# A hand-written TensorE order for the first column tiles of a four-sublayer diffusion backbone, with squares and modulated inputs shared differently between VectorE and ScalarE

## The chip, the cores and the metric

The kernel runs on one core of a Trainium2 chip. The metric is the device time of one execution in microseconds. TensorE (PE) does the matmuls, PEld is its weight load, VectorE is DVE, ScalarE is ACT, and SyncE (SP) issues the transfers. Times inside an execution are counted from the first instruction of its profile.

## The reference

Two layers work on 256 latent tokens and 256 context tokens of width 1024. What matters here is the very beginning of layer 0:

```python
mod_l = [m[..., None, :] for m in jnp.split(sc @ w_ada[l] + b_ada[l], 6, axis=-1)]   # sc = silu(c)
mod_c = [m[..., None, :] for m in jnp.split(scc @ w_ada[l] + b_ada[l], 6, axis=-1)]  # scc = silu(c_ctx)
hl = rms_norm(x, norm1_gain[l]) * (1.0 + mod_l[1]) + mod_l[0]
hc = rms_norm(z, norm1_gain[l]) * (1.0 + mod_c[1]) + mod_c[0]
... even_mixer(hc @ w_in_even[j], hl @ w_in_even[j], ...)
```

So each token is divided by its root mean square over the 1024 features, each feature is scaled and shifted by numbers that come from a product with `w_ada`, and the result `h` is multiplied by the wide input weight. Attention, two gated scans and two SwiGLU blocks follow; the change leaves their code alone.

## The kernel before, in words

Features lie on the partitions. The 1024 features make eight tiles `x[0]` to `x[7]` of 128 partitions by 512 tokens (256 context, 256 latent). In the instruction lists `x_86` or `x0_86` is `x[0]`, `x_88` is `x[1]`, and so on to `x_100`, which is `x[7]`.

**Precision.** Every dense product is made of three matmuls (`mm3`, L275): a float32 operand is split into a rounded high part and the low rest, and high times high, high times low and low times high are added. For weights, `wpiece` (L263) loads a 0.5 MB piece of eight 128x128 blocks into `w`, ScalarE rounds it to `wH` (L269) and VectorE subtracts to get `wL` (L270). There are four buffers of each. `Flat` (L280) hands the blocks out in order.

**The first stage** (L400 to L434) does this, for all eight feature tiles:

- 30 idle matmuls on `ones` (`keep_warm`, L397; a second call runs 6 on `rsd` later).
- Squares of the eight `x` tiles on ScalarE, four buffers; VectorE adds them in pairs; four matmuls with `ones` sum over the partitions into `nms`. `rstd_from_ms` (L254) takes Ln and then Exp on ScalarE; the result `rsd` is named `nrs` in the trace.
- The modulation of feature tile `dt` (`ada_first`, L182, through `ada_two`, L151): 16 small matmuls of `sc` with a 1 MB piece of `w_ada` (called the sums below; the trace counts 32 instructions), a copy `ada_ev` on ScalarE (L159), two transposes on TensorE (L161), and three small operations on VectorE that leave shift and scale in `modt` (L162, L165, L168).
- For each feature tile `k`: `x[k]` times `rsd` on VectorE (L424), scale and shift by halves on ScalarE (L427), rounding to `hH` on ScalarE (L429), subtraction to `hL` on VectorE (L430), then 18 matmuls of 512 columns: three for each of six output column tiles `pss[0]` to `pss[5]`, all accumulated over `k`. These six are the first column tiles.

Six weight pieces `w_even_a` serve this stage: piece 0 holds the blocks for `k` = 0 and the first two of `k` = 1, piece 1 goes on from there, and so on.

**The order.** Within an engine, instructions run in the order of the program. That order is made at build time by a scheduler that works with its own estimate of durations; `after` (L55) and `high_priority` only bend it. All transfers are issued from SP's queue, in an order that the scheduler also sets. Eight semaphores are handed to the transfers in turn, and a transfer is issued only once the one that had its semaphore before has landed.

Of the kernel before, what the change touches and what calls it, by code (L numbers as in the profile page):

```python
# [10 lines left out]
F32 = mybir.dt.float32  # L11
F32R = mybir.dt.float32r
U32 = mybir.dt.uint32
AF = mybir.ActivationFunctionType
ALU = mybir.AluOpType
# [3 lines left out]
P = 128  # L19
D = 1024  # L20
KT = D // P
NC_ = 256
T = 512
# [9 lines left out]
HOLD0 = (-1, -1, 1, 3)  # L33
HOLD1 = (-1, 1, 2, 4)
WARM1 = 30
WARM2 = 6
OUT = (KT, P, 256)
JOINT = "natural_log_exp_and_others"

# [11 lines left out]
def hybrid_kernel(ctx: ExitStack, tc: tile.TileContext, A, out, dbg=None):  # L51
    nc = tc.nc
    PE, V = nc.tensor, nc.vector

    def after(ins, deps):  # L55
        for d in deps:
            tc.add_manual_dep(
                ins.ins, d.ins.name, mybir.DependencyInfo(mybir.DependencyClass.NoSync, mybir.DependencyReason.DATA),
                reason="table order",
            )  # L60
# [27 lines left out]
    S = Act()  # L88

    def pool(es, name, bufs, **kw):  # L90
        kw.setdefault("reuse_waits", "tile")
        return es.enter_context(tc.tile_pool(name=name, bufs=bufs, **kw))

    cst = pool(ctx, "cst", 1)
# [9 lines left out]
    def dma(o, i):  # L104
        nc.sync.dma_start(out=o, in_=i)

    def load(name, shape, dt=F32, p=None):
        t = (p or cst).tile(list(shape), dt, name="c_" + name)
        dma(t, A[name])
        return t  # L110
# [5 lines left out]
    def mm(o, l, r, start, stop):  # L116
        return PE.matmul(out=o, lhsT=l, rhs=r, start=start, stop=stop)  # L117

    def mtile(name, tag):
        return pm.tile([P, 512], F32, name=name, tag=tag, bufs=1 if tag == "t" else 2)  # L120


    cc = load("cc", (P, KT, 2))
    ones = cst.tile([P, P], F32, name="ones")
    V.memset(ones, 1.0)
    x = {}
# [7 lines left out]
    ident = cst.tile([P, P], F32, name="ident")  # L134
    bada = cst.tile([P, 2, 6, KT], F32, name="bada")
    ngain = cst.tile([P, 2, 2, KT], F32, name="ngain")
    eps_t = cst.tile([P, 1], F32, name="eps_t")
    V.memset(eps_t, EPS)
    one_t = cst.tile([P, 1], F32, name="one_t")
# [7 lines left out]
    acoef = {}  # L147

    modt = mp.tile([P, 2, 6, KT, 2], F32, name="modt")

    def ada_two(ws, md, bias, gain, tag):  # L151

        ps = dtile() if tag == "d" else mtile("ada_ps", tag)
        for i, w in enumerate(ws):
            for j in range(2):
                for g in range(4):
                    mm(ps[32 * g:32 * g + 32, i * P:(i + 1) * P], sc[:, 2 * g + j, :], w[:, 2 * g + j, :], j == 0, j == 1)
        ev = mp.tile([P, 2 * P], F32, name="ada_ev", tag="ada_ev", bufs=2)
        S.copy(out=ev, in_=ps[:, 0:2 * P])  # L159
        for i in range(2):  # L160
            PE.transpose(ps[:, (2 + i) * P:(3 + i) * P], ev[:, i * P:(i + 1) * P], ident)  # L161
        V.tensor_reduce(  # L162
            out=md, in_=ps[:, 2 * P:4 * P].rearrange("p (i g r) -> p i r g", i=2, g=4)[:, :, 0:2, :], axis=AX.X, op=ALU.add
        )
        V.tensor_tensor(out=md, in0=md, in1=bias.unsqueeze(2).to_broadcast([P, 2, 2]), op=ALU.add)  # L165
        if gain is not None:
            md, gain = gain
            V.scalar_tensor_tensor(out=md, in0=md, scalar=1.0, in1=gain, op0=ALU.add, op1=ALU.mult)  # L168
# [7 lines left out]

    def ada_load(dt):
        w = nps.tile([P, 2, KT, P], F32, name="ada_w0", tag="ada_w0", bufs=4)
        dma(w, A["w_ada"][0, 0:2, dt].rearrange("m p k c -> p m k c"))
        return w  # L180

    def ada_first(dt, w):  # L182

        ada_two([w[:, 0], w[:, 1]], modt[:, 0, 0:2, dt, :], bada[:, 0, 0:2, dt],
                (modt[:, 0, 1, dt, :], ngain[:, 0, 0, dt:dt + 1].to_broadcast([P, 2])), "at"[dt % 2])

    pending = [(m, dt) for m in (2, 4, 3) for dt in range(0, KT, 2)]

# [55 lines left out]
    def halves(n):  # L244
        return ((0, 0, 256), (1, 256, 512)) if n == 512 else ((1, 0, 256),)

    def h_tiles(k, n, name, hpool):
        return (hpool.tile([P, n], F32R, name=f"{name}H{k}", tag=f"hH{k}"),
                hpool.tile([P, n], F32R, name=f"{name}L{k}", tag=f"hL{k}"))

    def shift(l, which, k, v):
        return mods[l, 3 * which, k][:, v:v + 1]

    def rstd_from_ms(o, ps, n):  # L254

        S.activation(out=o, in_=ps, func=AF.Ln, scale=1.0 / n, bias=eps_t)
        S.activation(out=o, in_=o, func=AF.Exp, scale=-0.5)
# [17 lines left out]
    def mm3(o, aH, aL, bH, bL, first, last):  # L275
        mm(o, aH, bH, first, False)
        mm(o, aH, bL, False, False)
        mm(o, aL, bH, False, last)
# [75 lines left out]
    def dtile():  # L354
        return pd.tile([P, 512], F32, name="d", tag="d")
# [3 lines left out]
    nps = pool(nes, "nps0", 2)  # L359
# [35 lines left out]
    def keep_warm(n, rhs):  # L395
        for _ in range(n):
            mm(idle[:, 0:rhs.shape[1]], ones, rhs, True, True)  # L397

    keep_warm(WARM1, ones)
    ms = mtile("nms", "s")  # L400
    for k in range(0, KT, 2):
        sq = [nps.tile([P, T], F32, name="nsq", tag="nsq", bufs=4) for _ in range(2)]
        for i in range(2):
            S.activation(out=sq[i], in_=x[k + i], func=AF.Square)
        V.tensor_tensor(out=sq[0], in0=sq[0], in1=sq[1], op=ALU.add)
        mm(ms, ones, sq[0], k == 0, k == KT - 2)
    rsd = nps.tile([P, T], F32, name="nrs0", tag="nrs0", bufs=1)
    rstd_from_ms(rsd, ms, D)
    keep_warm(WARM2, rsd[:, 0:256])
    aw = ada_load(0)  # L410
    dma(ident, A["ident"])
    dma(bada, A["b_ada"])
    dma(ngain, A["ngain"])
    fl = Flat(A["w_even_a"])
    fl.fetch()
    ada_first(0, aw)
    ada_first(1, ada_load(1))
    pss = [dtile(), dtile(), dtile(), mtile("d3", "s"), mtile("d4", "s"), mtile("d5", "a")]
    h = {}
    prev = []  # L420
    for k in range(KT):
        if 1 <= k < KT - 1:
            ada_first(k + 1, ada_load(k + 1))
        after(V.tensor_tensor(out=x[k], in0=x[k], in1=rsd, op=ALU.mult), prev)  # L424
        h[k] = h_tiles(k, T, "h", hp)
        for v, lo, hi in halves(T):
            xs = x[k][:, lo:hi]  # L427
            S.activation(out=xs, in_=xs, func=AF.Identity, scale=acoef[0, 0, k][:, v:v + 1], bias=shift(0, 0, k, v))
            S.copy(out=h[k][0][:, lo:hi], in_=xs)  # L429
            prev = [V.tensor_tensor(out=h[k][1][:, lo:hi], in0=xs, in1=h[k][0][:, lo:hi], op=ALU.subtract)]  # L430
        for ps in pss:
            wH, wL = fl.nxt()
            mm3(ps, wH, wL, h[k][0], h[k][1], k == 0, k == KT - 1)
    nes.close()  # L434
    hf = dict(x)

    mk32 = load("mk32", (P, 64), U32)
    mks = load("mks", (P, 5, 32), U32)
    gains = load("gains", (P, 3))
    onesw = one_t.to_broadcast([P, 256])  # L440
# [358 lines left out]
    for j in range(4):  # L799
        gs[j] = bigp.tile([P, T], F32, name=f"gs{j}", tag=f"vB{j}")  # L800
        ps = dtile()
# [17 lines left out]
    nps = pool(nes, "nps", 2)  # L819
# [12 lines left out]
    def close_norm(fl, rhs, ks, l, m, xs, ssq, nl, which):  # L832


        hs = {k: h_tiles(k, T, "h", hp2) for k in range(KT)}

        def part(v, ps):
            lo, hi = halves(T)[v][1:]
            for i, j in enumerate((KT - 2, KT - 1)):
                V.scalar_tensor_tensor(  # L840
                    out=xs[j][:, lo:hi], in0=ps[:, i * 256:(i + 1) * 256], scalar=mods[l, m, j][:, v:v + 1],
                    in1=xs[j][:, lo:hi], op0=ALU.mult, op1=ALU.add,
                )
# [16 lines left out]
    pss = [dtile(), dtile(), dtile(), mtile("d3", "t")]  # L860
# [64 lines left out]
    h = ffn(0, T, h, x, gpool, ssq, A["w_ffn_in0"], A["w_ffn_out0"])  # L925
# [213 lines left out]
    h = {k: h_tiles(k, 256, "h", hp2) for k in range(KT)}  # L1139
# [161 lines left out]
```

## Time and profile before

| what | value |
|---|---|
| three timed runs | 1173.56, 1174.69, 1174.72 us; median 1174.69 |
| the profiled execution | 1171.33 us, its span 1169.6 us |
| TensorE busy | 1146.2 us, 98% of the span |
| VectorE, ScalarE busy | 794.5 us (68%), 546.6 us (47%) |
| mean granted TensorE clock | 0.991 |
| end of the first column tiles on TensorE | 66.7 us from the start |

The profiled execution is 3.36 us shorter than the median of the timed runs. A timeline row reads: start, length, engine, line, operation, result and operands, and in brackets how long the engine sat idle before it and what ended that. Neighbouring instructions overlap a little, so the pitch of a series is shorter than the length of one.

### The profile page before, as it was taken

The page shows a single profiled execution, that of the slowest core. Times are in us where ns is not written, and L with a number is a line of the kernel's source. Part 1 is how long each engine was busy: PE and PEld are TensorE (multiplying, and loading weights), DVE is VectorE, ACT ScalarE, POOL GpSimd, SP SyncE. Part 2 cuts the span into 40 slices and gives each one's busy share as a digit, 9 for nine tenths or more (in the row PEclk, how much of TensorE's full clock was granted, in tenths as well). Part 3 has the DMA queues.
Part 4 walks back from the last instruction along what each step waited for, and adds up shares of the span by engine and source line. Part 5 has one row for each costly group of instructions (what it writes and reads, how often), then busy time and mean ns, then how long its engine had stood idle before and what let it go on. Part 6 is the DMA issues. An engine that isn't in the chain of part 4 may idle for free. (4 is left out here: it accounts for less than half of the span.)

```text
span 1169.6 us, 21851 instructions
## 1 busy us (share of the span) xinstructions
PE 1146.2 (98%) x8954; PEld 982.8 (84%) x8954; DVE 794.5 (68%) x1671; ACT 546.6 (47%) x952; POOL 0.2 (0%) x4
## 2 busy tenths in 40 slices
PE   8999999999999999999999999999999998999998
PEld 6777665666889888888888889999898988999998
DVE  3537856985767767666677637869899976655663
ACT  5436546754435222212222325958778865433432
POOL 0000000000000000000000000000000000000000
PEclk9999989999999999999999999999999999999999
DMA  9531432234423555555776422342221234555552
GB/s 356 211 116 36 146 127 82 100 127 146 178 74 105 167 178 171 159 174 179 252 238 232 161 90 70 129 145 92 73 91 61 87 127 129 183 191 178 185 181 91
DMA packets 50021, 170.19 MB, mean 146 GB/s; under 512 B 6528, under 2 KB 8064, under 8 KB 49792
## 3 DMA queue, kind: packets, MB, share of 16 engines
q1 hardware_dynamic: 49920, 168.79, 43.2%
q8 instruction: 70, 1.15, 0.4%
q14 instruction: 31, 0.25, 0.1%
HBM read 167.72 MB, written 1.05 MB: 144 GB/s over the span
## 5 line engine op out<-in xcount | busy, mean ns | idle before, releaser
L269 ACT CAST wH<-w 128x1024 fp32r<-128x1024 f32 x212 | 222.2, 1049 | 410.2 <-PE d L117 314.0
L117 PE MATMUL d<-hL,wH 128*128 128x256 f32 (+1 forms) x1152 | 386.7, 336 | 2.5 <-DVE hL L387 2.5
L117 PE MATMUL d<-hH,wH 128*128 128x256 f32 (+1 forms) x1152 | 382.4, 339 | 5.6 <-ACT hH L71 4.1
L117 PE MATMUL d<-hH,wL 128*128 128x256 f32 (+1 forms) x1152 | 385.3, 335 | 0.0
L270 DVE TENSOR_TENSOR wL<-w,wH 128x1024 fp32r<-128x1024 f32 x212 | 258.6, 1221 | 124.7 <-ACT wH L269 122.0
L117 PEld LDWEIGHTS d<-hH,wH 128*128 128x128 f32 x1152 | 218.3, 191 | 32.0 <-ACT hH L71 4.9
L117 PEld LDWEIGHTS d<-hL,wH 128*128 128x128 f32 x1152 | 220.6, 191 | 25.0 <-DVE hL L387 3.3
L117 PEld LDWEIGHTS d<-hH,wL 128*128 128x128 f32 x1152 | 220.1, 191 | 21.5
L117 PE MATMUL d<-gL,wH 128*128 128x256 f32 (+1 forms) x374 | 121.8, 327 | 0.0
L117 PE MATMUL d<-gH,wL 128*128 128x256 f32 (+1 forms) x374 | 121.7, 327 | 0.0
L117 PE MATMUL d<-gH,wH 128*128 128x256 f32 (+1 forms) x374 | 121.7, 327 | 0.0
L227 DVE SCALAR_TENSOR_TENSOR jk<-ada_w,scb 128x1024 bf16<-128x1024 f32 x80 | 97.7, 1222 | 2.2 <-DMA ada_w<-in_w_ada 0.8
L882 DVE TENSOR_TENSOR fs<-fs,d 128x256 f32<-128x256 f32 (+1 forms) x46 | 24.6, 536 | 77.4 <-PE d L117 75.8
L117 PEld LDWEIGHTS d<-gL,wH 128*128 128x128 f32 x374 | 71.1, 190 | 6.1
L117 PEld LDWEIGHTS d<-gH,wL 128*128 128x128 f32 x374 | 71.1, 190 | 6.0
L117 PEld LDWEIGHTS d<-gH,wH 128*128 128x128 f32 x374 | 71.0, 190 | 6.0
L117 PE MATMUL d<-wH,hH 128*128 128x256 f32 (+1 forms) x192 | 61.9, 323 | 0.0
L117 PE MATMUL d<-wL,hH 128*128 128x256 f32 (+1 forms) x192 | 61.6, 322 | 0.0
L117 PE MATMUL d<-wH,hL 128*128 128x256 f32 (+1 forms) x192 | 61.5, 321 | 0.0
L825 DVE SCALAR_TENSOR_TENSOR x<-d,modt,x 128x256 f32<-128x256 f32 x64 | 28.5, 480 | 42.4 <-PE d L117 42.4
L71 ACT ACTIVATE QK<-QK 128x512 f32<-128x512 f32 x72 | 42.6, 628 | 2.4 <-DVE QK L493 2.1
L117 PEld LDWEIGHTS a<-QK 128*32 128x32 f32 (+5 forms) x1408 | 33.8, 118 | 10.1 <-issue 6.3
(216 smaller groups left out, 1461.1 us busy)
## 6 DMA issues: line engine op xcount, KB each, us to landing
w<-in_w_ffn_in SPq DMA_DIRECT2D x88, 512.0 KB, 3.4
ada_w<-in_w_ada SPq DMA_DIRECT2D x80, 512.0 KB, 4.2
w<-in_w_ffn_out SPq DMA_DIRECT2D x44, 512.0 KB, 3.4
ada_w<-in_w_ada SPq DMA_DIRECT2D x8, 1024.0 KB, 9.4
w<-in_w_even_a SPq DMA_DIRECT2D x16, 512.0 KB, 4.8
w<-in_w_odd_f SPq DMA_DIRECT2D x16, 512.0 KB, 3.3
x<-in_xT SPq DMA_DIRECT2D x16, 256.0 KB, 3.7
w<-in_w_out_even SPq DMA_DIRECT2D x8, 512.0 KB, 3.5
```

The source lines that it names most:

```text
L71: ins = nc.scalar.activation(**kw)
L117: return PE.matmul(out=o, lhsT=l, rhs=r, start=start, stop=stop)
L227: ins = V.scalar_tensor_tensor(out=jk, in0=w1[0], scalar=1.0, in1=scb[:, v, :], op0=ALU.mult, op1=ALU.mult, accum_out=modt[:, l, m, dt, v: ...
L269: S.copy(out=wH, in_=w)
L270: ins = V.tensor_tensor(out=wL, in0=w, in1=wH, op=ALU.subtract)
L825: tail[0] = V.scalar_tensor_tensor(out=xt[:, lo:hi], in0=ps[:, lo:hi], scalar=mods[l, m, k][:, v:v + 1], in1=xt[:, lo:hi], op0=ALU.mult, o ...
L882: V.tensor_tensor(out=s[:, lo:hi], in0=s[:, lo:hi], in1=pu, op=ALU.mult)
```

## The change

- TensorE's order is taken out of the scheduler's hands from the first idle matmul to the last matmul of the first column tiles (`manual_schedule`): it is the order of the code. The other engines' orders still come from the scheduler.
- `ada_two` is cut in `ada_sums` and `ada_turn`. The sums of tile `k + 2` stand in the middle of the matmuls of tile `k`, as do the turn (transposes and VectorE's three operations) and `h` of tile `k + 1`.
- Squares 1, 4 and 6 are made by VectorE, the other five by ScalarE; every square has a buffer of its own, and five instead of four matmuls sum them.
- Scale and shift of `h` move from ScalarE to VectorE; `hL` is one operation of 512 columns instead of two of 256.
- `cc`, `ident`, `b_ada` and `ngain` are issued from ScalarE's queue; each 1 MB piece of `w_ada` is loaded in two transfers.
- Six idle matmuls on `rsd` become two on the last square and three on `rsd`.

```diff
+    def dma_act(o, i):
+        nc.scalar.dma_start(out=o, in_=i)
...
-    cc = load("cc", (P, KT, 2))
+    cc = cst.tile([P, KT, 2], F32, name="c_cc")
+    dma_act(cc, A["cc"])
...
+    dma_act(ident, A["ident"])
+    dma_act(bada, A["b_ada"])
+    dma_act(ngain, A["ngain"])
...
     def ada_load(dt):
         w = nps.tile([P, 2, KT, P], F32, name="ada_w0", tag="ada_w0", bufs=4)
-        dma(w, A["w_ada"][0, 0:2, dt].rearrange("m p k c -> p m k c"))
+        for m in range(2):
+            dma(w[:, m], A["w_ada"][0, m, dt])
         return w
...
+    ordered = ExitStack()
+    ordered.enter_context(tc.manual_schedule(engines={PE.engine}))
     keep_warm(WARM1, ones)
     ms = mtile("nms", "s")
-    for k in range(0, KT, 2):
-        sq = [nps.tile([P, T], F32, name="nsq", tag="nsq", bufs=4) for _ in range(2)]
-        for i in range(2):
-            S.activation(out=sq[i], in_=x[k + i], func=AF.Square)
-        V.tensor_tensor(out=sq[0], in0=sq[0], in1=sq[1], op=ALU.add)
-        mm(ms, ones, sq[0], k == 0, k == KT - 2)
+    sq = [nps.tile([P, T], F32, name=f"nsq{k}", tag=f"nsq{k}", bufs=1) for k in range(KT)]
+    for k in range(KT):
+        if k in (1, 4, 6):
+            V.tensor_tensor(out=sq[k], in0=x[k], in1=x[k], op=ALU.mult)
+        else:
+            S.activation(out=sq[k], in_=x[k], func=AF.Square)
+    for k in (0, 2, 4):
+        V.tensor_tensor(out=sq[k], in0=sq[k], in1=sq[k + 1], op=ALU.add)
+    for k in (0, 2, 4, 6, 7):
+        mm(ms, ones, sq[k], k == 0, k == KT - 1)
     rsd = nps.tile([P, T], F32, name="nrs0", tag="nrs0", bufs=1)
     rstd_from_ms(rsd, ms, D)
-    keep_warm(WARM2, rsd[:, 0:256])
...
+    first_sums(0)
+    keep_warm(2, sq[KT - 1][:, 0:256])
+    first_turn(0)
+    keep_warm(3, rsd[:, 0:256])
...
+    def first_h(k):
+        V.tensor_tensor(out=x[k], in0=x[k], in1=rsd, op=ALU.mult)
+        h[k] = h_tiles(k, T, "h", hp)
         for v, lo, hi in halves(T):
             xs = x[k][:, lo:hi]
-            S.activation(out=xs, in_=xs, func=AF.Identity, scale=acoef[0, 0, k][:, v:v + 1], bias=shift(0, 0, k, v))
+            V.tensor_scalar(out=xs, in0=xs, scalar1=acoef[0, 0, k][:, v:v + 1], scalar2=shift(0, 0, k, v),
+                            op0=ALU.mult, op1=ALU.add)
             S.copy(out=h[k][0][:, lo:hi], in_=xs)
-            prev = [V.tensor_tensor(out=h[k][1][:, lo:hi], in0=xs, in1=h[k][0][:, lo:hi], op=ALU.subtract)]
-        for ps in pss:
+        V.tensor_tensor(out=h[k][1], in0=x[k], in1=h[k][0], op=ALU.subtract)
+
+    first_h(0)
+    for k in range(KT):
+        if k + 2 < KT:
+            aws[k + 2] = ada_load(k + 2)
+        for j, ps in enumerate(pss):
+            if k == 0 and j == 2:
+                first_sums(1)
+            if j == (4 if k == 0 else 2):
+                if k + 1 < KT:
+                    first_turn(k + 1)
+                    first_h(k + 1)
+                if k + 2 < KT:
+                    first_sums(k + 2)
             wH, wL = fl.nxt()
             mm3(ps, wH, wL, h[k][0], h[k][1], k == 0, k == KT - 1)
+    ordered.close()
```

The names below carry buffer numbers; `x0` to `x7` are the feature tiles, `hH0` and `hL0` the two parts of `h[0]`, `nrs0` is `rsd`.

VectorE, from the first weight subtraction on, before:

```order
L270 TENSOR_TENSOR wL_190<-w_187,wH_189 128x1024
L162 TENSOR_REDUCE modt_112<-ada_ps_193 128x2x2
L424 TENSOR_TENSOR x0_86<-x0_86,nrs0_172 128x512
L165 TENSOR_TENSOR modt_112<-modt_112,bada_103 128x2x2
L168 SCALAR_TENSOR_TENSOR modt_112<-modt_112,ngain_104 128x2
L430 TENSOR_TENSOR hL0_251<-x0_86,hH0_250 128x256 x2
L424 TENSOR_TENSOR x1_88<-x1_88,nrs0_172 128x512
```

and in the changed kernel:

```order
L287 TENSOR_TENSOR wL_187<-w_184,wH_186 128x1024
L445 TENSOR_TENSOR x0_86<-x0_86,nrs0_177 128x512
L445 TENSOR_TENSOR x1_88<-x1_88,nrs0_177 128x512
L445 TENSOR_TENSOR x2_90<-x2_90,nrs0_177 128x512
L445 TENSOR_TENSOR x3_92<-x3_92,nrs0_177 128x512
L445 TENSOR_TENSOR x4_94<-x4_94,nrs0_177 128x512
L445 TENSOR_TENSOR x5_96<-x5_96,nrs0_177 128x512
L445 TENSOR_TENSOR x6_98<-x6_98,nrs0_177 128x512
L445 TENSOR_TENSOR x7_100<-x7_100,nrs0_177 128x512
L174 TENSOR_REDUCE modt_115<-ada_ps_193 128x2x2
L177 TENSOR_TENSOR modt_115<-modt_115,bada_103 128x2x2
L180 SCALAR_TENSOR_TENSOR modt_115<-modt_115,ngain_104 128x2
```

All eight products with `rsd` now stand ahead of the first tile's scale and shift; before, only that of `x[0]` did.

ScalarE, from the last square to the rounding of `h[1]`, before:

```order
L71 ACTIVATE nsq_167<-x7_100 128x512
L269 CAST wH_189<-w_187 128x1024
L71 ACTIVATE nrs0_172<-nms_147,eps_t_105 128x512
L159 COPY ada_ev_210<-ada_ps_193 128x256
L71 ACTIVATE nrs0_172<-nrs0_172 128x512
L71 ACTIVATE x0_86<-x0_86,modt_112 128x256 x2
L429 CAST hH0_250<-x0_86 128x256 x2
L269 CAST wH_319<-w_317 128x1024
L159 COPY ada_ev_236<-ada_ps_219 128x256
L269 CAST wH_384<-w_382 128x1024
L159 COPY ada_ev_295<-ada_ps_278 128x256
```

and in the changed kernel:

```order
L70 ACTIVATE nsq7_160<-x7_100 128x512
L286 CAST wH_186<-w_184 128x1024
L70 ACTIVATE nrs0_177<-nms_152,eps_t_108 128x512
L70 ACTIVATE nrs0_177<-nrs0_177 128x512
L168 COPY ada_ev_210<-ada_ps_193 128x256
L451 CAST hH0_229<-x0_86 128x256 x2
L286 CAST wH_351<-w_349 128x1024
L286 CAST wH_416<-w_414 128x1024
L286 CAST wH_484<-w_482 128x1024
L168 COPY ada_ev_262<-ada_ps_245 128x256
L168 COPY ada_ev_300<-ada_ps_283 128x256
L451 CAST hH1_276<-x1_88 128x256 x2
```

The rounding of weight piece 0 stays ahead of Ln (the first `nrs0` row); the roundings of pieces 1, 2 and 3 now all stand ahead of `ada_ev_262`, the copy that the second tile's transposes need.

TensorE, in the middle of tile 0, before:

```order
L117 MATMUL d5_248<-hH0_250,wL_190 128x512
L117 MATMUL ada_ps_278<-ada_w0_276,sc_109 32x128 x8
L161 MATMUL ada_ps_219<-ident_102,ada_ev_236 128x128 x2
L117 MATMUL ada_ps_278<-ada_w0_276,sc_109 32x128 x8
L117 MATMUL ada_ps_337<-ada_w0_335,sc_109 32x128 x16
L161 MATMUL ada_ps_278<-ident_102,ada_ev_295 128x128 x2
L161 MATMUL ada_ps_337<-ident_102,ada_ev_354 128x128 x2
L117 MATMUL d_243<-hH1_303,wH_189 128x512
```

and in the changed kernel:

```order
L119 MATMUL d3_225<-hH0_229,wL_187 128x512
L173 MATMUL ada_ps_245<-ident_102,ada_ev_262 128x128 x2
L119 MATMUL ada_ps_283<-ada_w0_236,sc_112 32x128 x16
L119 MATMUL d4_226<-hH0_229,wH_186 128x512
L119 MATMUL d4_226<-hL0_230,wH_186 128x512
L119 MATMUL d4_226<-hH0_229,wL_187 128x512
L119 MATMUL d5_227<-hH0_229,wH_186 128x512
```

Before, the sums and transposes for the next tiles came in one block after tile 0's matmuls; now the transposes of tile 1 and the sums of tile 2 stand ahead of tile 0's last six matmuls.

## Rows read from the trace of the kernel before

**Rows 1.** The page's first part: busy time, share and instructions of each engine.

```profile
PE 1146.2 (98%) x8954; PEld 982.8 (84%) x8954; DVE 794.5 (68%) x1671; ACT 546.6 (47%) x952; POOL 0.2 (0%) x4
```

**Rows 2.** Busy time of engines by stretch; last three columns: clock, DMA share, GB/s.

```profile
5.00:10.00 5.00, 5.00 (x45) 4.89 (x44) 2.08 (x3) 4.08 (x8) 0.00 (x0) 1.00 1.00 358
...
20.00:25.00 5.00, 5.00 (x53) 3.59 (x54) 1.68 (x2) 1.32 (x2) 0.00 (x0) 1.00 1.05 401
...
45.00:50.00 5.00, 5.00 (x43) 3.79 (x42) 1.22 (x1) 1.41 (x2) 0.00 (x0) 1.00 0.29 93
```

**Rows 3.** Timeline of TensorE, first 73 us: start, length, line, operation, idle before.

```profile
13.46 1.12 PE L117 MATMUL nms<-nsq,ones 128*128 128x512 f32 x2
...
16.03 0.44 PE L161 MATMUL ada_ps<-ident,ada_ev 128*128 128x128 f32 x2 [1.10 <-ACT ada_ev L159]
16.56 2.86 PE L117 MATMUL idle<-nrs,ones 128*128 128x256 f32 x12
19.42 1.65 PE L117 MATMUL d<-hH,wH 128*128 128x512 f32 x6
21.00 1.08 PE L117 MATMUL ada_ps<-ada_w,sc 128*32 128x128 f32 x32
...
29.45 0.44 PE L161 MATMUL ada_ps<-ident,ada_ev 128*128 128x128 f32 x2 [1.67 <-ACT ada_ev L159]
...
58.45 1.52 PE L117 MATMUL d<-hH,wH 128*128 128x512 f32 x6
...
62.53 1.52 PE L117 MATMUL d<-hH,wH 128*128 128x512 f32 x6
...
66.71 0.38 PE L117 MATMUL lps<-lpr,ones 64*128 64x2 f32 x2
...
72.91 1.92 PE L117 MATMUL lr_ps<-x,c_w_lr 128*32 128x512 f32 x16
```

**Rows 4.** Timeline of ScalarE, first 30 us.

```profile
14.08 1.04 ACT L269 CAST wH<-w 128x1024 fp32r<-128x1024 f32 x1 [2.70 <-DMA w<-in_w_even_a]
15.03 0.68 ACT L71 ACTIVATE nrs<-nms,eps_t 128x512 f32<-128x512 f32 x1
15.61 0.36 ACT L159 COPY ada_ev<-ada_ps 128x256 f32<-128x256 f32 x1
15.86 0.64 ACT L71 ACTIVATE nrs<-nrs 128x512 f32<-128x512 f32 x1
...
18.67 0.69 ACT L429 CAST hH<-x 128x256 fp32r<-128x256 f32 x2
...
25.89 1.05 ACT L269 CAST wH<-w 128x1024 fp32r<-128x1024 f32 x1 [2.56 <-DMA w<-in_w_even_a]
```

**Rows 5.** Timeline of SP's queue, first 14 us: issues of transfers.

```profile
0.73 0.39 SPq L105 DMA_DIRECT2D c_cc<-in_cc  x1
1.18 3.74 SPq L105 DMA_DIRECT2D x<-in_xT  x8
```

**Rows 6.** Timeline of VectorE, first 54 us.

```profile
15.16 1.23 DVE L270 TENSOR_TENSOR wL<-w,wH 128x1024 fp32r<-128x1024 f32 x1 [3.05 <-ACT wH L269]
...
16.68 0.69 DVE L424 TENSOR_TENSOR x<-x,nrs 128x512 f32<-128x512 f32 x1
...
19.09 0.76 DVE L430 TENSOR_TENSOR hL<-x,hH 128x256 fp32r<-128x256 f32 x2 [1.45 <-ACT hH L429]
...
51.35 0.17 DVE L162 TENSOR_REDUCE modt<-ada_ps 128x4 f32<-128x16 f32 x1 [3.83 <-PE ada_ps L161]
51.55 0.17 DVE L165 TENSOR_TENSOR modt<-modt,bada 128x4 f32<-128x4 f32 x1
51.75 0.16 DVE L168 SCALAR_TENSOR_TENSOR modt<-modt,ngain 128x2 f32<-128x2 f32 x1
```

**Rows 7.** Groups of VectorE's instructions by line and shape: busy us, mean ns.

```profile
L765 DVE TENSOR_SCALAR p<-p,st 128x256 f32<-128x256 f32 x8 | 2.7, 343 | 0.0
```

**Rows 8.** Stretches with a lower granted clock; columns as in rows 2.

```profile
162.00:163.00 1.00, 0.26 (x2) 0.12 (x1) 0.90 (x6) 1.00 (x5) 0.00 (x0) 0.50 0.74 299
163.00:164.00 1.00, 0.76 (x2) 0.67 (x3) 0.90 (x5) 0.62 (x1) 0.00 (x0) 0.50 0.97 389
...
171.00:172.00 1.00, 1.00 (x4) 0.75 (x3) 0.73 (x4) 0.23 (x1) 0.00 (x0) 0.50 0.45 61
172.00:173.00 1.00, 1.00 (x6) 0.82 (x5) 0.17 (x1) 0.79 (x4) 0.00 (x0) 0.90 0.87 311
```

More of the change, by code (lines that the diff above doesn't have):

```diff
@@ L35 @@
 WARM1 = 30
-WARM2 = 6
 OUT = (KT, P, 256)
@@ L151, in ada_two, with ada_sums @@
     def ada_two(ws, md, bias, gain, tag):
+        ada_turn(*ada_sums(ws, tag), md, bias, gain)
+    def ada_sums(ws, tag):
         ps = dtile() if tag == "d" else mtile("ada_ps", tag)
@@ L159, in ada_two, with ada_turn @@
         S.copy(out=ev, in_=ps[:, 0:2 * P])
+        return ps, ev
+    def ada_turn(ps, ev, md, bias, gain):
         for i in range(2):
@@ L178, in ada_load, with first_sums, first_turn @@
         w = nps.tile([P, 2, KT, P], F32, name="ada_w0", tag="ada_w0", bufs=4)
-        dma(w, A["w_ada"][0, 0:2, dt].rearrange("m p k c -> p m k c"))
-        return w
-    def ada_first(dt, w):
-        ada_two([w[:, 0], w[:, 1]], modt[:, 0, 0:2, dt, :], bada[:, 0, 0:2, dt],
-                (modt[:, 0, 1, dt, :], ngain[:, 0, 0, dt:dt + 1].to_broadcast([P, 2])), "at"[dt % 2])
+        for m in range(2):
+            dma(w[:, m], A["w_ada"][0, m, dt])
+        return w
+    def first_sums(dt):
+        w = aws.pop(dt)
+        sums[dt] = ada_sums([w[:, 0], w[:, 1]], "at"[dt % 2])
+    def first_turn(dt):
+        ada_turn(*sums.pop(dt), modt[:, 0, 0:2, dt, :], bada[:, 0, 0:2, dt],
+                 (modt[:, 0, 1, dt, :], ngain[:, 0, 0, dt:dt + 1].to_broadcast([P, 2])))
     pending = [(m, dt) for m in (2, 4, 3) for dt in range(0, KT, 2)]
@@ L397, in keep_warm @@
             mm(idle[:, 0:rhs.shape[1]], ones, rhs, True, True)
+    ordered = ExitStack()
+    ordered.enter_context(tc.manual_schedule(engines={PE.engine}))
     keep_warm(WARM1, ones)
     ms = mtile("nms", "s")
-    for k in range(0, KT, 2):
-        sq = [nps.tile([P, T], F32, name="nsq", tag="nsq", bufs=4) for _ in range(2)]
-        for i in range(2):
-            S.activation(out=sq[i], in_=x[k + i], func=AF.Square)
-        V.tensor_tensor(out=sq[0], in0=sq[0], in1=sq[1], op=ALU.add)
-        mm(ms, ones, sq[0], k == 0, k == KT - 2)
+    sq = [nps.tile([P, T], F32, name=f"nsq{k}", tag=f"nsq{k}", bufs=1) for k in range(KT)]
[8 more added lines that the diff above has]
+        mm(ms, ones, sq[k], k == 0, k == KT - 1)
     rsd = nps.tile([P, T], F32, name="nrs0", tag="nrs0", bufs=1)
     rstd_from_ms(rsd, ms, D)
-    keep_warm(WARM2, rsd[:, 0:256])
[L410 to L413, printed above, removed]
+    aws, sums = {}, {}
+    aws[0] = ada_load(0)
     fl = Flat(A["w_even_a"])
     fl.fetch()
-    ada_first(0, aw)
-    ada_first(1, ada_load(1))
+    aws[1] = ada_load(1)
+    first_sums(0)
+    keep_warm(2, sq[KT - 1][:, 0:256])
+    first_turn(0)
+    keep_warm(3, rsd[:, 0:256])
     pss = [dtile(), dtile(), dtile(), mtile("d3", "s"), mtile("d4", "s"), mtile("d5", "a")]
     h = {}
[L420 to L424, printed above, removed]
+    def first_h(k):
+        V.tensor_tensor(out=x[k], in0=x[k], in1=rsd, op=ALU.mult)
         h[k] = h_tiles(k, T, "h", hp)
```

## The prediction

> **What bounds the kernel now.** Read the busy shares first: TensorE is at 98% of the span [rows 1], so a change pays only by what it takes out of TensorE's line. Next the stretches of the first 70 us: the DMA engines are full (share 1.00 to 1.05) from 5 to past 25 us and at 0.29 by 45 us [rows 2], so early on the transfers set when work can begin, and later TensorE does. Then the timelines. On TensorE the stage has an opening (idle matmuls, sums of squares) up to 19.42, and from there the matmuls of the eight tiles, which end at 66.7 [rows 3]: 47.3 us. On ScalarE the opening hangs on one transfer: the rounding of weight piece 0 waits for its DMA until 14.08 and Ln stands behind it at 15.03 [rows 4], although the engine had sat idle for 2.70 us.
>
> What 47.3 us are made of: 18 matmuls of a tile take 62.53 - 58.45 = 4.08 us, the sums of one tile 1.08 us [rows 3], with a switch to and fro some 1.2; two transposes add about 0.25 beyond what overlaps. 8 x 4.08 + 7 x 1.2 + 7 x 0.25 = 42.8 us. So some 4.5 us of waits and gaps lie in the stage, the longest 1.67 us behind a copy of ScalarE [rows 3]. That, and the opening, is all a better order can win here.
>
> **The change part by part.**
>
> *Constants on ScalarE's queue.* SP's first x transfer is issued at 1.18 instead of 0.73 because `cc` stands ahead of it [rows 5]. Moving `cc` brings x forward by 0.45 us. The other three constants still move their bytes on engines that are full [rows 2], and before the first weight piece as before. So piece 0 lands at 14.08 - 0.45 = 13.6. Splitting the `w_ada` pieces moves the same bytes; eight more issues of some 0.43 us on SP are covered while transfers queue. What four issues cost ScalarE no row shows; by SP's rows 0.4 us each, 0 at least, and they stand where ScalarE waits for `cc` anyway.
>
> *Squares.* Sharing them and giving each a buffer can end the sums of squares before 14.58 (13.46 + 1.12 [rows 3]); the fifth matmul costs at most 1.1 us (the length of the last pair of rows [rows 3]) of an otherwise idle opening. But Ln still stands behind the rounding of piece 0. That ends at 13.6 + 1.04, so Ln begins at 14.6 (0.95 after the rounding began, as at 15.03 [rows 4]), and Exp ends 1.47 - 0.25 = 1.2 us later, since the copy that stood between them now follows. `rsd` is there at 15.8 instead of 16.5. Of all that was done for the squares 0.7 us remains.
>
> *The first h.* On VectorE all eight products with `rsd` now precede the first tile's modulation. One takes 0.69 us; two neighbours of 0.42 take 0.76, so they overlap by 0.08 [rows 6]: 0.69 + 7 x 0.61 = 5.0 us, to 20.8. The three small operations take 0.56 (51.35 to 51.91 [rows 6]): 21.4. Scale and shift on VectorE: the nearest row is a TENSOR_SCALAR of 128x256, 343 ns [rows 7], two in 0.6 us: 22.0; at ScalarE's old length it would be up to 1.1. The second rounding ends 0.4 us on (two took 0.69 [rows 4]). First matmul at **22.5 instead of 19.42**: 3.1 us later. `hL` is one operation of 0.69 now, so the second matmul waits to 23.2.
>
> *Tile 0.* Five more matmuls, the sums of tile 1 and six matmuls bring TensorE to 26.9. Then come the transposes of tile 1. Their copy stands on ScalarE behind the roundings of pieces 1 to 3. Piece 2 was waited for until 25.89 [rows 4]; piece 3 is another 0.52 MB at 401 GB/s [rows 2], so 27.2 before; the bytes ahead of it are the same now, so 26.75. Rounding and copy, 0.95 + 0.4: the copy is done at 28.1. TensorE waits 1.2 us. This also says that the late start costs little in itself: tile 0 is held by piece 3 in either case. Transposes, sums of tile 2 and six matmuls: 30.9. The subtraction for piece 3 (1.23 [rows 6]) stands before tile 1's modulation on VectorE, so `hL1` comes at 31.4 and costs another 0.25.
>
> *Tiles 1 to 7.* From then on the chain transposes, modulation, scale, rounding, `hL` (0.4 + 0.56 + 0.6 + 0.4 + 0.7 = 2.7 us, or 3.9 with a weight subtraction of 1.23 in between) has 1.2 + 12 x 0.227 = 3.9 us of TensorE work beside it. It just fits; without that cover each tile would wait up to 1.2. Tiles 1 to 5: 5 x (4.08 + 1.2 + 0.25) = 27.7; if the transposes overlap and switches are cheap, 5 x 5.3 = 26.5. Tile 6 without sums 4.35, tile 7 0.4 + 4.08 (its rounding stands behind one more weight rounding). The low-rank matmuls `lr_ps`, 1.9 us at 72.91 before [rows 3], now stand inside tile 7 and cover the wait for `hL7`; they are only moved.
>
> *Sum.* 30.9 + 0.25 + 27.7 + 4.35 + 4.5 = 67.7, or 66.4 with the cheaper tiles, against 66.7. The stage ends **0.3 us earlier to 1.0 later**; I take 0.6 later: of the 4.5 us of gaps before, one row explains 1.67, so switches may well cost more than I set them at. On the profiled execution that gives 1171.33 + 0.6 = 1171.9; on the median, which lies 3.36 higher, **1175.3**. A difference under 0.2% (2.35 us) is what a measurement of this kernel can't tell from no change, so the forecast is "same".
>
> *What is reordered behind.* From 67 to about 330 us the scheduler has dealt the scan and attention steps out anew on all three engines. TensorE's line goes on bounding the time there; its weakest spot is the run of small matmuls ahead of 162, after which the clock fell [rows 8]. No row prices the new order; I take nothing for it. Its ends: one low stretch less or more, worked out below.
>
> **The rivals.**
>
> *Slower: the hole before the first matmul lets the clock fall.* The three idle matmuls on `rsd` take half of the 2.86 us that six took [rows 3], so TensorE ends them near 17.5 and does nothing until 22.5. Before, the opening's hole was 1.10 us [rows 3]. From 162 to 172, after thin work, the granted clock was 0.50, that is 1.2 instead of 2.4 GHz, and stayed so for 8 us in which TensorE was busy again [rows 8]. If that happens here, the 4.2 us of work before the second tile's transposes take 8.4: 31.4 instead of 28.1, and the next microseconds lose some more: 4 us, 1179. It decides when the low clock outlasts the 1.2 us that TensorE would wait anyway, so a low stretch of 2 to 3 us costs nothing. The Trainium skill (TensorE: Matmul & The Clock Gate, on oscillation in real kernels) says that an idle gap between bursts throttles the array and the next burst starts at half clock; by that rule the fall here is certain, and rows 8 agree that thin work brings it. For: the hole is over four times that of the old opening. Against: tile 0 has slack. With a late piece 3 (each microsecond counts in full) I give the slower side 0.30.
>
> *Faster: the reordered stretch keeps its clock.* From 163 to 172 TensorE worked at half clock [rows 8]; at full clock those 9 us of work take some 4.4 less. If the new order puts dense matmuls between the small ones there, 1175.3 - 4.4 = 1171. For: tile 0's shift and the new order change which matmuls meet. Against: the changed order still has two runs of small matmuls with few dense ones among them. Together with an earlier piece 3 and smaller gaps between tiles: 0.30.
>
> *The change doesn't do what it says.* The sharing of squares is hidden behind piece 0's transfer and the hand order by piece 3's: this is part of the forecast. Were Ln not held, `rsd` could come near 13 and the first matmul near 19.5; tile 0 would still wait for 28.1, so the end would not move.
>
> **How the numbers follow.** Forecast, within 2.35 us of the median: 0.40. Slower 0.30, around 1179. Faster 0.30, around 1171. The forecast's own range is 1173.5 to 1177. The range of 8 in 10 reaches into both other cases: down to 1169.4 (the kept clock on the lower sum, 1170.0, less half the 1.2 us that the three runs spread), up to 1180.0 (the low clock on the upper sum, 1179.4, and the same half).
>
> **What would show it.** Right: eight products with `rsd` in a row on VectorE from about 15.9; first dense matmul at 22 to 23; a wait of TensorE for the second tile's copy, ended near 28; end of the tiles (without `lr_ps`) at 66 to 68. Wrong: a first matmul before 20 and tiles that run through without that wait, or a granted clock of 0.50 beyond 27 us; and in the stretches from 120 to 330 us more or less time at 0.50 than the 10 us seen now.

## The result, and the profile after

The changed kernel takes **1184.63 us** (median of four runs, 1182.05 to 1187.3) against 1174.12 for the kernel before: ratio 1.0096, 95% interval 1.0072 to 1.0121. It is about 10.5 us slower. The forecast was "no difference", 1175.3, and the time lies outside its range. The profiled execution took 1186.04 us, with a span of 1184.2.

First the busy times by stretch. Columns: the stretch, its length, TensorE, its weight load, VectorE, ScalarE, GpSimd; then the granted clock, the DMA share and GB/s. Of the kernel before:

```profile
0.00:70.00 70.00, 65.26 (x511) 49.73 (x512) 30.32 (x73) 37.02 (x69) 0.20 (x4) 1.00 0.71 263
70.00:380.00 310.00, 301.97 (x2634) 224.88 (x2633) 213.07 (x573) 158.86 (x311) 0.00 (x0) 0.98 0.33 111
380.00:700.00 320.00, 320.00 (x1441) 266.22 (x1440) 210.48 (x319) 75.48 (x85) 0.00 (x0) 1.00 0.56 183
```

And of the changed kernel:

```profile
0.00:70.00 70.00, 63.90 (x503) 47.91 (x504) 36.72 (x83) 25.47 (x45) 0.20 (x4) 0.95 0.72 263
70.00:380.00 310.00, 293.14 (x2551) 218.55 (x2551) 202.76 (x556) 154.63 (x307) 0.00 (x0) 0.96 0.31 103
380.00:700.00 320.00, 320.00 (x1438) 266.08 (x1437) 216.57 (x328) 79.70 (x90) 0.00 (x0) 1.00 0.57 186
```

From 380 to 700 us TensorE is full in both. The loss lies ahead of that, in two places. In the first 70 us TensorE idles 1.4 us more and its clock is lower. From 70 to 380 us it idles 16.9 instead of 8.0 us, and the clock is lower there too. One norm sum further down, at the same place of both programs, shows the total. It starts at 705.75 in the timeline of TensorE before, and at 720.90 after, 15.15 us later in these two executions:

```profile
705.75 0.59 PE L117 MATMUL nms<-ssq,ones 128*128 128x256 f32 x2
```

```profile
720.90 0.59 PE L119 MATMUL nms<-ssq,ones 128*128 128x256 f32 x2
```

**The first stage.** The timeline of TensorE after, to hold against [rows 3]:

```profile
17.03 0.44 PE L173 MATMUL ada_ps<-ident,ada_ev 128*128 128x128 f32 x2 [0.38 <-ACT ada_ev L168]
17.30 1.46 PE L119 MATMUL idle<-nrs,ones 128*128 128x256 f32 x6
23.39 0.79 PE L119 MATMUL d<-hH,wH 128*128 128x512 f32 x1 [4.63 <-ACT hH L451]
...
26.55 1.94 PE L119 MATMUL ada_ps<-ada_w,sc 128*32 128x128 f32 x32
...
30.51 0.38 PE L173 MATMUL ada_ps<-ident,ada_ev 128*128 128x128 f32 x2
...
65.98 0.38 PE L119 MATMUL lps<-lpr,ones 64*128 64x2 f32 x2
...
66.71 1.92 PE L119 MATMUL lr_ps<-x,c_w_lr 128*32 128x512 f32 x16
...
72.55 1.02 PE L119 MATMUL g_ps<-lr,c_w_up 128*128 128x512 f32 x2
```

The first dense matmul starts at 23.39 instead of 19.42. The last column tile ends at 72.55; less the 1.86 us by which `lr_ps` inside it puts off the next matmul, that is 70.7 against 66.7. So the stage itself ends 4.0 us later, and from its first dense matmul on it takes 47.3 us, as before. What held the first matmul stands in VectorE's timeline after ([rows 6] before):

```profile
16.75 4.91 DVE L445 TENSOR_TENSOR x<-x,nrs 128x512 f32<-128x512 f32 x8
21.57 0.17 DVE L174 TENSOR_REDUCE modt<-ada_ps 128x4 f32<-128x16 f32 x1
...
22.17 0.74 DVE L449 TENSOR_SCALAR x<-x,modt 128x256 f32<-128x256 f32 x2
```

Eight products in a row stand ahead of the first modulation, whose transposes had ended at 17.5. TensorE is empty meanwhile. Then its granted clock falls to 0.50, that is 1.2 instead of 2.4 GHz, as busy times of two microseconds each show:

```profile
22.00:24.00 2.00, 0.61 (x1) 0.28 (x1) 1.49 (x4) 1.23 (x3) 0.00 (x0) 0.73 1.02 405
24.00:26.00 2.00, 2.00 (x6) 1.49 (x5) 1.43 (x3) 1.59 (x2) 0.00 (x0) 0.50 1.08 385
26.00:28.00 2.00, 2.00 (x30) 1.36 (x32) 1.97 (x5) 1.04 (x1) 0.00 (x0) 0.50 1.03 412
28.00:30.00 2.00, 2.00 (x16) 1.38 (x9) 0.67 (x2) 0.37 (x1) 0.00 (x0) 0.56 1.03 410
```

**Behind the first stage.** The list of TensorE's waits from 70 to 380 us after (who waited for whom: total, times, longest):

```profile
PE d L119 <- DVE wL L287: 3.9, 1, 3.9
PE d L119 <- DVE oH L664: 3.4, 1, 3.4
PE s_ps L119 <- ACT p L70: 3.4, 2, 3.1
PE d L119 <- ACT hH L70: 2.0, 1, 2.0
```

The same list before begins with the line that is fourth here; nothing above it:

```profile
PE d L117 <- ACT hH L71: 2.0, 1, 2.0
PE a L117 <- issue: 1.2, 1, 1.2
```

So three waits of 3.1 to 3.9 us are new. Each comes from the order on an engine. The first, on ScalarE:

```profile
134.62 1.04 ACT L286 CAST wH<-w 128x1024 fp32r<-128x1024 f32 x1 [1.34 <-DMA w<-in_w_even_a]
...
136.37 0.47 ACT L70 ACTIVATE p<-s_ps,st 128x256 f32<-128x256 f32 x1
```

The attention's exponential `p` stands behind a weight rounding that waits for its transfer, and TensorE, which needs the buffer that `p` frees, idles 3.14 us to 136.98. The second is on VectorE: the low half `wL` of a weight piece comes at 207.52, behind differences of the score building, though its rounding ended at 202.65. For the third, one sum over channels (`ms_ps`) starts at 315.44 amid dense matmuls, so the gates and the split `oH` behind it come too late for the matmul at 321.52.

The clock belongs to the account too. Behind each of the three waits the granted clock is at 0.50 for a while; from 160 to 172 us it is at 1.00, where before it was at 0.50 from 162 on [rows 8]. Of the changed kernel:

```profile
138.00:140.00 2.00, 2.00 (x4) 0.50 (x3) 2.00 (x10) 1.63 (x3) 0.00 (x0) 0.50 0.55 188
160.00:172.00 12.00, 12.00 (x331) 8.83 (x330) 9.23 (x32) 6.00 (x12) 0.00 (x0) 1.00 0.28 90
210.00:212.00 2.00, 2.00 (x7) 1.54 (x6) 2.00 (x8) 1.03 (x3) 0.00 (x0) 0.50 0.61 231
324.00:326.00 2.00, 2.00 (x6) 1.52 (x6) 2.00 (x4) 0.00 (x0) 0.00 (x0) 0.50 0.00 0
```

A further low stretch, from 285 to 292 us, has no long wait ahead of it; what brings it is open.

### The profile page after: what moved, and what is told of

It reads as the page before. It is cut to its first block, busy times and chain, and to the rows that moved or that the text cites. A ratio compares the mean times of both kernels' runs of the same rounds, so it can differ in the third digit from the quotient of the medians.

```text
span 1184.2 us, 21861 instructions
## 1 busy us (share of the span) xinstructions
PE 1151.3 (97%) x8954; PEld 988.1 (83%) x8954; DVE 802.1 (68%) x1681; ACT 538.7 (45%) x933; POOL 0.2 (0%) x4
## 5 line engine op out<-in xcount | busy, mean ns | idle before, releaser
L119 PE MATMUL d<-hH,wH 128*128 128x256 f32 (+1 forms) x1152 | 389.7, 341 | 9.0 <-ACT hH L451 4.6
```

## The experiments

Behind the first stage both programs hold the same instructions in the same program order (9689 of them on the four engines that the scheduler orders: TensorE, VectorE, ScalarE and SyncE's transfers); only the scheduler's deal differs. So that deal can be written down and held: for each of the four a table of instruction numbers, and an edge of order (no semaphore) from each to the next:

```diff
+        for a, b in zip(seq[:-1], seq[1:]):
+            tc.add_manual_dep(
+                tail[b], tail[a].name,
+                mybir.DependencyInfo(mybir.DependencyClass.NoSync, mybir.DependencyReason.DATA),
...
```

This makes first stage and order behind it two factors that can be crossed. **Theory A:** the order is most of the loss, the first stage the smaller part. **Rival B:** the new stage leaves something behind that costs the rest. **Rival C:** the order alone costs all of it. All runs were timed in five rounds beside the kernel before, whose median was 1173.25 (experiments 1 to 4), 1173.31 (5 to 8), 1172.91 (9 to 12) and 1172.71 (13 to 16).

### 1 and 2: stage and order, crossed

The changed kernel with the table of the kernel before, and the other way round.

> The changed first stage as it stands; behind it all four engines that the scheduler orders (TensorE, VectorE, ScalarE and SyncE's transfers) are held in the order of the kernel before, instruction for instruction. Theory A (the first stage as written costs about 4 us by its late start and the half clock behind it, the rest is the order that the scheduler deals behind it): median 1178, 1176.5 to 1179.5. Rival B (the new first stage leaves something behind, buffers, queues or a transfer order, that costs the rest too): 1183 to 1186, as the changed kernel. Rival C (the order alone costs all 10): 1174.

> The first stage of the kernel before, and behind it the four engines held in the order that the changed kernel has there. Theory A: 1174 plus the 6 us that the first stage does not explain, 1179 to 1182. Rival B: 1174, as before, since the order is not what costs. Rival C: 1184. If A and the first experiment hold, the two differences from the kernel before add up to about 10.5.

Measured: new stage with old order **1174.61** (1.0014, 1.0003 to 1.0025); old stage with new order **1182.22** (1.0076, 1.0055 to 1.0096). Rival B falls. Of the 10.5 us the order makes about 9, the stage 1.4. So the stage cost less than theory A had it (1176.5 to 1179.5), and these two alone hardly part A from rival C: the stage's share is 0.4 to 2.9 us by its interval. In the first experiment's profile the dense work still starts at 23.06 and `lr_ps` is 2.9 us later than before, and only part of that reaches the end. The waits in the second experiment's profile are the changed kernel's:

```profile
PE d L117 <- DVE wL L270: 3.9, 1, 3.9
PE s_ps L117 <- ACT p L71: 3.9, 3, 3.3
PE d L117 <- DVE oH L628: 3.4, 1, 3.4
```

### 3, 4 and 8: the first stage, with the old order held behind it

```diff
-        V.tensor_tensor(out=x[k], in0=x[k], in1=rsd, op=ALU.mult)
+        after(V.tensor_tensor(out=x[k], in0=x[k], in1=rsd, op=ALU.mult), turn)
...
-            V.tensor_scalar(out=xs, ...)
+            turn[:] = [V.tensor_scalar(out=xs, ...)]
```

> As the first of these, and each product of x by the inverse deviation is held behind the two modulations of the tile before it, so that the eight products no longer stand ahead of the first modulation. Theory A: modulation 0 is ready at about 18 instead of 22.1, the first dense matmul starts near 19.4, the clock does not fall, and of the 4 us about 3.5 to 4 come back: 1174 to 1175 in all. Rival D (piece 0 of the weights or the sums of tile 1 hold the dense work anyway): 1177 to 1178, as the first.

Measured: **1170.38** (0.9974, 0.9963 to 0.9985): 4.2 less than the first experiment, under the kernel before and below both spans. Its VectorE:

```profile
16.59 0.69 DVE L445 TENSOR_TENSOR x<-x,nrs 128x512 f32<-128x512 f32 x1 [0.25 <-ACT nrs L70]
17.57 0.17 DVE L174 TENSOR_REDUCE modt<-ada_ps 128x4 f32<-128x16 f32 x1 [0.28 <-PE ada_ps L173]
...
18.17 0.73 DVE L449 TENSOR_SCALAR x<-x,modt 128x256 f32<-128x256 f32 x2
18.82 0.68 DVE L445 TENSOR_TENSOR x<-x,nrs 128x512 f32<-128x512 f32 x1
```

Modulation 0 is there 4 us earlier, the first dense matmul starts at 19.40, and the clock stays at 1.00 through the stage. The edit moved one thing more: the scheduler dealt ScalarE's queue in the stage anew, and the copy for the second tile now stands ahead of the rounding of piece 1 instead of behind that of piece 3:

```profile
22.65 0.37 ACT L168 COPY ada_ev<-ada_ps 128x256 f32<-128x256 f32 x1 [3.31 <-PE ada_ps L119]
23.57 1.05 ACT L286 CAST wH<-w 128x1024 fp32r<-128x1024 f32 x1 [0.55 <-DMA w<-in_w_even_a]
```

What of the 4.2 us belongs to the products and what to this copy was not parted.

To part the hole from the clock, the hole was filled with idle matmuls (`keep_warm(3, ...)` became 20, then 11):

> As the first of these, with 20 warming matmuls ahead of the first dense one instead of 3, so that TensorE works through its idle 18.8 to 23.4 us on a scratch sum; the start of the dense work stays where it is. Theory A: the granted clock stays at 1.00 from 22 to 30 us, which gives back the 2.8 us read for it in the changed kernel: 1175 to 1176. If the fall of the clock does not matter to the end (what bounds 23 to 30 us is VectorE or the pieces), it stays at 1178.

> The fourth experiment again with its number of warming matmuls right: those took 0.49 us each, so 20 of them ended at 25.8 us and not at 23.4. 11 of them end near 22.5. Theory A: the clock stays at 1.00 from 22 to 30 us; of the 1.4 us that the new stage costs with the order before, what the half clock costs comes back: 1172 to 1173.5. If the clock's fall costs nothing at the end: 1174.6, as the first experiment.

Measured: 1175.35 (1.0017, 1.0007 to 1.0026) and 1177.64 (1.0033, 1.0021 to 1.0045): no gain. In both profiles the clock does stay at 1.00. With 20 the dense work began at 25.43, too late for a fair test. With 11 it began at 23.00, and `lr_ps` came at 75.23 instead of 75.78, so between these two executions holding the clock gave 0.55 us at the end of the stage; 2.8 had been expected. (In the first experiment's execution the clock was at 0.50 only from 24 to 26 us and at 0.78 in the next two.) With 11 the total was 2 to 3 us worse than in the first experiment all the same. Its profile has a gap of 2.70 us ahead of modulation sums at 134.89 that the first experiment's has not. Why that comes with warm matmuls 110 us earlier is open.

### 5, 10, 11 and 12: the three waits

In the held table of the changed kernel seven instructions move: two on VectorE and two on ScalarE for the wait at 134 us; one `wL` on VectorE for that at 205; one sum on TensorE and, on ScalarE, one rounding behind the Ln and Exp for that at 318.

> The changed kernel's first stage and its own order behind it, with seven instructions moved: two negated maxima on VectorE and two exponentials of the attention on ScalarE forward, past six differences of the score building and past a weight rounding that waits for its transfer (the 3.1 us wait at 134 us); the low half of one weight piece on VectorE forward, past eight differences and two small ones (the 3.9 us wait at 205); one sum over 128 channels on TensorE 18 rows forward, and the Ln and Exp behind it on ScalarE past one rounding (the 3.4 us wait at 318). Theory A1 (the loss is in these three in-order waits, 10.4 us of idle TensorE, and in the low clock behind each): 1174 to 1178. Rival A2 (the loss is spread over the order, and the next late instruction takes over at each place): 1181 to 1185.

Measured: **1171.92** (0.9988, 0.998 to 0.9997), 12.7 us under the changed kernel, whose first stage it still has, and 2 us below the span of A1. Rival A2 falls. The waits left, from 70 to 380 us:

```profile
PE d L119 <- ACT hH L70: 2.0, 1, 2.0
PE d L119 <- DMA ada_w<-in_w_ada: 1.5, 1, 1.5
PE d L119 <- DVE modt L174: 1.2, 1, 1.2
```

It is also 2.7 us faster than the first experiment, which has the same stage and the old order, and the intervals of the two don't meet (0.998 to 0.9997, 1.0003 to 1.0025). So without its three waits the new order is the better one. The clock fits that: between 120 and 330 us it is clearly below 1.00 only from 137 to 141 in this profile, and from 166 to 174 in the first experiment's. That this is all of the 2.7 us isn't shown.

Each alone:

> The changed kernel with its own order held and of the seven moves those of the wait at 134 us alone: two negated maxima on VectorE, two exponentials on ScalarE. Theory A1 (each wait costs its own idle time, here 3.1 us, and the low clock behind it, about 1 to 2): 1179.5 to 1182. Rival A3 (the waits hang together: the first one shifts what is behind it, and the others go with it): 1172 to 1176. Rival A4 (alone it only moves the wait further on): 1184 to 1186.

> As the tenth, with the one move of the wait at 205 us alone: the low half of one weight piece on VectorE ahead of ten small instructions. Theory A1: 3.9 us of idle and 1 to 2 of low clock come back, 1179 to 1181. Rival A4: 1184 to 1186.

> As the tenth, with the moves of the wait at 318 us alone: one sum over channels 18 rows forward on TensorE, Ln and Exp ahead of one rounding on ScalarE. Theory A1: 3.4 us of idle and 1 to 2 of low clock come back, 1179 to 1181.5. Rival A4: 1184 to 1186. If A1 holds for all three, their gains add up to the 12.7 us between the changed kernel and the fifth experiment.

Measured: 1180.37 (1.007, 1.0048 to 1.0092), 1179.44 (1.0057, 1.0039 to 1.0075) and 1177.88 (1.0042, 1.0029 to 1.0056): gains of 3.1, 4.6 and 6.3 us (by the ratios, from the changed kernel's 1.0096). In each profile the wait that was moved is gone or at most 0.4 us and the other two stand (the one on `p` at 3.5 and 4.5 us in the eleventh and twelfth), as in the tenth:

```profile
PE d L119 <- DVE wL L287: 4.3, 2, 3.9
PE d L119 <- DVE oH L664: 3.4, 1, 3.4
PE d L119 <- DVE modt L174: 2.3, 1, 2.3
```

A3 and A4 fall. The three add up to 14.0 where all together gave 12.7; with intervals of some 3 us on each, that is the same. It is more than the 10.4 us that TensorE idled there: the rest fits the low clock behind the waits, shown above. The 12.7 us are more than the order's 9, since the rest of the new order gains some 3.

### 6 and 13: which part of the change turns the order over

The build alone shows the order. Least number of TensorE's 7014 instructions behind the first stage that must move to get from one order to the other:

```
kernel                                         from before   from changed
before, squares shared as in the change               5          254
before, scale and shift on VectorE                    2          249
before, w_ada in two transfers                        1          250
before, cc alone on ScalarE's queue                   1          250
before, all four constants on ScalarE's queue       247           79
changed, its constants back on SP's queue           251           77
changed, scheduler orders TensorE throughout        247            6
changed, products of x in turn                      256           19
   the same, lr_ps held behind the stage             18          243
```

The scheduler deals in one of two ways here, and the four constants alone tip it from one to the other. Taking them back does not undo it. The other parts (squares, scale on VectorE, split transfers) leave the order, and were not run alone. The sixth experiment is the kernel before with this one edit:

```diff
+    for t, n in ((ident, "ident"), (bada, "b_ada"), (ngain, "ngain")):
+        nc.scalar.dma_start(out=t, in_=A[n])
...
-    dma(ident, A["ident"])
-    dma(bada, A["b_ada"])
-    dma(ngain, A["ngain"])
```

and `cc` likewise; the thirteenth is the same with the old order held.

> The kernel before with one part of the change alone: cc, ident, bada and ngain go out on ScalarE's queue, ahead of the first stage; the scheduler deals the rest freely. Its order behind the first stage then comes out close to the changed kernel's (77 to 79 of 7014 TensorE instructions stand otherwise than there, 247 otherwise than in the kernel before). Theory A: the first stage is that of before, and the time is that of the dealt order, 1179 to 1185. Rival (the order costs only together with the changed first stage): 1173 to 1176.

> As the sixth experiment (the kernel before, its four constants on ScalarE's queue), with everything behind the first stage held in the order of the kernel before. Theory A (the queue costs through the order it makes the scheduler deal, little by itself): 1173 to 1176. Rival Q (the queue costs by itself: cc lands later, and the transfers of w_ada and the pieces come in another order): 1178 or more, of the 12 us that the sixth experiment lost.

Measured: **1185.16** (1.0098, 1.0083 to 1.0113) with the scheduler free, **1172.82** (1.0003, 0.9987 to 1.0018) with the old order held. Rival Q falls. Four transfers moved to another queue cost 12 us, and none that shows by themselves, though `lr_ps` came at 75.03 in the thirteenth's profile, 2.1 us later than before. The waits of the sixth, from 70 to 380 us:

```profile
PE s_ps L117 <- ACT p L71: 4.3, 4, 3.1
PE d L117 <- DVE wL L273: 3.9, 1, 3.9
PE d L117 <- DVE oH L628: 3.4, 1, 3.4
```

What in the constants tips the scheduler wasn't found.

### 14: the constants in the changed stage

> As the first experiment (the changed first stage, the order before behind it), with cc, ident, b_ada and ngain back on SyncE's queue, in their old place. If the late landing of cc (3.93 against 2.43 us) and the four issues on ScalarE delay the stage, it comes earlier by 0.5 to 1: 1173.5 to 1174.2. If the stage hangs on piece 0 of the weights alone: 1174.6, as the first, or up to 0.5 more.

Measured: 1175.25 (1.0019, 1.0005 to 1.0033), as the first experiment within the intervals. Both lie clear of the kernel before, if only just, so the stage costs something of its own and rival C falls. Where the constants are issued makes no difference to the stage that shows.

### 7 and 15: repairs with the scheduler free

Products in turn, and in the seventh the `lr_ps` matmuls held behind the last column tile as well:

```diff
-            mm(lr_ps[32 * g:32 * g + 32, :], ...)
+            after(mm(lr_ps[32 * g:32 * g + 32, :], ...), [tail7])
```

> The changed kernel with the products of x in turn and nothing else; the scheduler deals the rest freely, and deals it as in the changed kernel but for 19 of 7014 TensorE instructions. Theory A: the stage's 4.2 us come back (first against third experiment) and the order's 9 stay: 1179 to 1182. Rival: the earlier end of the stage lets the waits at 134, 205 and 318 us close by themselves: 1170 to 1174.

> The changed kernel with two edges of order and no table: the products of x in turn, as in the third experiment, and the eight matmuls of lr_ps held behind the last matmul of the column tiles instead of inside tile 7; the scheduler deals the rest freely, and deals it nearly as in the kernel before (18 of 7014 TensorE instructions stand otherwise). Theory A: 1169.5 to 1172, as with the order held by a table (1170.4). If the order held by a table owed its time to something else than the order (a longer chain of dependences, other waits), it is 1176 or more.

Measured: 1177.08 (1.0051, 1.0031 to 1.0072) and **1170.54** (0.9981, 0.9971 to 0.9992). Products in turn alone keep the three waits (3.0, 3.9 and 3.4 us in its profile) and most of the order's loss. The result lies 2 us below the expected span; by the ratios 5.3 us came back, and the 4.2 expected are within the intervals. With the second edge the scheduler deals nearly as before, and the time is that of the held table (1170.38). So the table itself costs or brings nothing that shows.

### 9 and 16: both repairs, a kernel faster than both

> The products of x in turn (third experiment) together with the changed kernel's own order with seven instructions moved (fifth): both repairs at once. The fifth measured 1171.9 with the late start still in it, and holding the products was worth 4.2 from the first to the third. Theory A (the two losses lie in different stretches and add): 1167 to 1169. Rival (the clock or the next wait gives part of it back): 1170 to 1172.

> The ninth experiment (products in turn, seven instructions moved, 1166.6) with the four constants back on SyncE's queue. If the constants on ScalarE's queue are a gain or a loss of the stage by themselves, it shows here in the best version: 1166.6 plus or minus 1 if they are neither.

Measured: **1166.58** (0.9955, 0.9939 to 0.9971) and **1167.17** (0.9954, 0.9937 to 0.9971). The losses add. The change's own order, with seven instructions moved and its products in turn, beats the kernel before by 0.45% (some 5 us) and, by the ratios, the changed kernel by some 17.

## Why the prediction was wrong

**The step that failed** is "What is reordered behind": "No row prices the new order; I take nothing for it", with one low stretch (4.4 us) as its ends. The order cost about 9 us (second experiment). The prediction looked there for a change of clock alone, and for thin runs of small matmuls on TensorE. The loss came from the order on VectorE and ScalarE, and in one place on TensorE itself: instructions that TensorE waits for stood behind others that wait or need no haste. The three waits were 3.1, 3.9 and 3.4 us long, and moving seven instructions gave back 12.7 us (fifth experiment). The build's lists of order show, without a run, which instruction stands ahead of which on these engines. Ten instructions of up to 0.4 us ahead of a `wL` could have been priced from them, and ends of 4.4 us were too narrow.

**Where the prediction sought the cause** was the first stage. By its own points:

- *"Moving `cc` brings x forward by 0.45 us", piece 0 at 13.6.* Wrong. The first x transfer was issued at 0.73, but the eight issues took 4.90 us instead of 3.74 [rows 5], so that what followed came later. Piece 0 was rounded from 14.42 in the changed kernel's profile and from 14.09 in the first experiment's, against 14.08 [rows 4].
- *Eight products in a row, to 20.8; first matmul at 22.5.* Right in mechanism and size: 4.91 us for the eight (5.0 forecast), the three small operations and the scaling as costed. All lay 0.8 to 0.9 us later, since piece 0 and with it Ln did.
- *"Tile 0 is held by piece 3 in either case"* and the 1.2 us wait near 28. The wait didn't come. The rounding of piece 3 ran from 26.07 to 27.11; the copy behind it began only at 28.55, when TensorE's own sums were done, and TensorE came to the transposes at 30.51. So the low clock and not piece 3 held tile 0. With the products in turn the copy no longer stood behind piece 3, `lr_ps` came 4.1 us earlier than in the first experiment, and the total was 4.2 us less.
- *The clock falls in the hole*, a rival with 0.30. It did: 0.50 from 24 to 28 us, after 4.63 us without work. The Trainium skill (TensorE: Matmul & The Clock Gate, on oscillation in real kernels) says that an idle gap between bursts throttles the array, and the trace agrees. But the tiles took 47.3 us in spite of it, as before: what the hand order saved between tiles the clock took (tile 0 up to the transposes took 7.1 us, in the third experiment at full clock 4.6). At the stage's end the price of 4 us was about right (4.0 us later in this profile), at the kernel's end overstated: with the old order the whole stage costs 1.4 us (0.4 to 2.9), which also takes in the 0.6 of the forecast.
- *The reordered stretch keeps its clock*, a rival with 0.30. From 160 to 172 us it did, at 1.00; the low clock behind the three new waits outweighed that.
- *"The change doesn't do what it says"*: with the products in turn the same hand order starts at 19.40 and the kernel gains 0.2 to 0.3%, so what it sets out to do works; the row of eight products and the order behind the stage hid it.

The outcome had the sign of the slower rival (1179), but that rival's mechanism was only the smaller part of it. It lies beyond the wider range too, whose upper end by its own terms is 1174.7 + 1.0 + 4.0 + 0.6 = 1180.3, not 1180.0.

## What to carry to other kernels

Where a scheduler deals an order from its own estimates, a small edit at the start may turn over hundreds of instructions far behind it: hold the old order once as a table and cross it with the edit, and you know which of the two you have timed. Read the dealt order on the engines that feed the bounding one, for a rounding that waits for a transfer ahead of something urgent. A new wait of the bounding engine cost here 1.0 to 1.9 times its length, with an uncertainty of some 3 us on each.

## What was not expected of the hardware

`cc` (8 KB), issued at 0.72 us on ScalarE's queue, landed at 3.93 us; issued at 0.73 as the first on SyncE's queue [rows 5], it landed at 2.43. The first table load of ScalarE waits for it in both (after, then before):

```profile
3.93 1.28 ACT L70 ACT_TABLE_LOAD   x1 [3.93 <-DMA c_cc<-in_cc]
```

```profile
2.43 1.28 ACT L71 ACT_TABLE_LOAD   x1 [2.43 <-DMA c_cc<-in_cc]
```

Nothing at the end of the stage followed from it (`lr_ps` at 75.78 in the first experiment, at 75.59 in the fourteenth with the constants on SyncE's queue).

The eight issues of x on SyncE's queue took longer while ScalarE issued its four transfers. After, to hold against [rows 5]:

```profile
0.73 4.90 SPq L104 DMA_DIRECT2D x<-in_xT  x8
```

It was 3.74 us before and in the fourteenth experiment, and 4.72 to 4.90 in the changed kernel and the first, third, sixth, eighth and thirteenth experiments.

An idle matmul of 256 columns in float32 took 0.49 us (three, as six instructions, in 1.46), and 20 of them took 8.80 us and outlasted the hole they were to fill.
